# Strassen's scheme for three quarters of an MLP's up projections in a two-layer diffusion step

## The chip, the cores and the metric

The kernel runs on one core of a Trainium2 chip. Its time is the device time of one execution in microseconds; the median of the runs is compared.

## The reference, cut to what matters

One inference step of a backbone with two trunk layers, on 640 tokens (512 latent tokens and 128 context tokens) of width 1024. Each layer has four token mixers, a gated merge, and an MLP with a squared ReLU:

```python
def squared_relu_mlp(h, w1, w2):
    return jnp.square(jax.nn.relu(h @ w1)) @ w2

x = x + gt2 * squared_relu_mlp(modulate(rms_norm(x, lw['g_mlp']), sh2, sc2), lw['w_ff1'], lw['w_ff2'])
```

`w1` is 1024 x 4096, `w2` 4096 x 1024, all in float32. The change is in `h @ w1` of the second of the two layers.

## The kernel before, in words

Channels lie on the 128 partitions and tokens along the free dimension. The 640 tokens are two halves of 320 (`HALF`), and a matmul moves one half. Float32 precision is made from three passes: each operand is a rounded high part and a low part (value minus high part), and `steps` (lines 216 to 231) does, for each of 8 chunks of 128 input channels, high x high (L226), high x low (L227) and low x high (L228). A slab of weights, 1024 inputs by 128 outputs, thus takes 8 x 3 x 2 halves = 48 matmuls of 320 columns. The trace calls the weights' parts `whi` and `wlo`, those of the MLP's input `hhi` and `hlo`, those of the hidden values `hh` and `hl`.

The weights come in one order, written down at the start by `plan` in the queue `feed`. `raw` (L167) starts the load of the next slab on SyncE's queue. `prefetch` (L174) makes a loaded slab's parts: the cast to the high part on ScalarE (L192), the subtract for the low part on VectorE (L193), and then it starts the next load. `take` (L198) hands out a ready slab and, through `look`, prepares one more. There are two buffers for prepared slabs: one in use by TensorE, and the next.

The MLP splits the 4096 hidden channels into four parts (`NQ`) of eight slabs (`QJ`). The order is: up of part 0, then for q = 1, 2, 3 up of part q and down of part q-1, then down of part 3. In `up` a slab takes, after its matmuls, four steps for each half: relu from PSUM on ScalarE (L1066), square on VectorE (L1067), and the split into high part on ScalarE (L240) and low part on VectorE (L241). The first two slabs of part 0 (`first`) are done in `Norm.second`, between the last steps of the norm. In `down` a half's result is added to x on VectorE by two operations (`residual`, L1008). The down of part 3 goes through `boundary`, which does the first token halves of all eight slabs, then the second halves with the final norm between them. The chunks of a down slab are the eight hidden slabs of the part, in order.

In the merge and the MLP, the instructions of VectorE, ScalarE, GpSimd and SyncE stand in the order in which the program issues them (`in_order`); TensorE's do so everywhere. PSUM has eight banks, one for a half's result.

Of the kernel before, what the change touches and what calls it, by code (L numbers as in the profile page):

```python
# [9 lines left out]
F32 = mybir.dt.float32  # L10
F32R = mybir.dt.float32r
AF = mybir.ActivationFunctionType
ALU = mybir.AluOpType
# [15 lines left out]
NQ = 4  # L29
QJ = DFF // NQ // P  # L30
# [42 lines left out]
def hsl(h):  # L73
    return slice(h * HALF, (h + 1) * HALF)


def _r(ap):
    return ap.bitcast(F32)


class Net:
    def __init__(self, ctx, nc, tc, t):
        self.nc, self.tc, self.t = nc, tc, t
        self.uid = 0
        pool = lambda name, **k: ctx.enter_context(tc.tile_pool(name=name, bufs=1, **k))
        self.cst = pool("cst", side="left")
        self.wp = pool("wp", side="left")
        self.hp = pool("hp", side="left")
        self.dr = pool("dr", space=DRAM)
        self.ydram = [self.dr.tile([10, P, NTOK], F32, name=f"ydram{l}") for l in range(DEPTH)]  # L90
        self.gdram = [self.dr.tile([len(EARLY_GATES[l]), P, NTOK], F32, name=f"gdram{l}") for l in range(DEPTH)]
        self.xdram = self.dr.tile([P, KC, NTOK], F32, name="xdram")
        self.pv = None
        self.wm = deque()
        self.feed, self.raws, self.ready = deque(), deque(), deque()
        for l in range(DEPTH):
            self.plan(l)
# [35 lines left out]
    def plan(self, l):  # L133
        t, f = self.t, self.feed
        wa = lambda c: f.append((t["wa"][l, c], KC, P, "w", True))
        gates = iter(EARLY_GATES[l])
        slabs = [GK, GQ, GV]
        for task in FILL[l]:
            slabs += task[1] + (GATE,) * task[2] if task else (GATE,)
        assert slabs.count(GATE) == len(EARLY_GATES[l])  # L140
        for c in slabs:
            if c == GATE:
                f.append((t["wg"][l][next(gates)], KC, P, "w", True))
            elif c == MKR:
# [12 lines left out]
        for j in range(KC):  # L157
            f.append((t["wo"][l, j], KC, P, "w", False))
        up = lambda q: [f.append((t["w1"][l, q * QJ + j], KC, P, "w", False)) for j in range(QJ)]
        down = lambda q: [f.append((t["w2"][l, q, j], KC, P, "w", False)) for j in range(KC)]  # L160
        up(0)
        for q in range(1, NQ):
            up(q)
            down(q - 1)
        down(NQ - 1)

    def raw(self):  # L167

        src, kc, m, tag, eng = self.feed.popleft()
        r = self.wp.tile([P, kc, m], F32, name="raw" + tag, tag="raw" + tag, bufs=2 if tag == "w" else 1)  # L170
        self.nc.sync.dma_start(r, src.rearrange("p (k m) -> p k m", k=kc))
        self.raws.append((r, kc, m, tag, eng))

    def prefetch(self, dst=None):  # L174

        nc = self.nc
        if not self.raws:
            self.raw()
        raw, kc, m, tag, eng = self.raws.popleft()
        if dst is None:  # L180
            hi, lo = (self.wp.tile([P, kc, m], F32R, name=n + tag, tag=n + tag, bufs=2 if tag == "w" else 1)
                      for n in ("whi", "wlo"))
        else:
            hi, lo = dst
        if eng and kc == KC:

            for a, e in ((0, nc.gpsimd), (KC // 2, nc.vector)):
                c = slice(a, a + KC // 2)
                nc.scalar.copy(hi[:, c], raw[:, c])  # L189
                e.tensor_tensor(lo[:, c], raw[:, c], _r(hi[:, c]), ALU.subtract)  # L190
        else:
            nc.scalar.copy(hi, raw)  # L192
            nc.vector.tensor_tensor(lo, raw, _r(hi), ALU.subtract)  # L193
        while self.feed and not self.raws or self.raws and self.feed and self.raws[-1][3] != "w" and self.feed[0][3] == "w":
            self.raw()
        self.ready.append((hi, lo, tag))

    def take(self, ahead=True, dst=None):  # L198

        if not self.ready:  # L200
            self.prefetch()
        hi, lo, tag = self.ready.popleft()
        if ahead:
            self.look(tag)
        return hi, lo

    def look(self, last="w"):

        while self.raws or self.feed:
            if self.ready:  # L210
                last = self.ready[-1][2]
                if last == "w":
                    return
            if last == "b" and (self.raws[0][3] if self.raws else self.feed[0][3]) == "b":
                return
            self.prefetch()
# [823 lines left out]
    def mlp(self, l, x, first):  # L1040
# [52 lines left out]
            down(q - 1)  # L1093
        down(NQ - 1)

    def start(self):

        nc, t = self.nc, self.t
        self.ps_stack = ExitStack()
        self.ps_stack.enter_context(self.psum(8))  # L1100
        xs = ExitStack()
        xp = xs.enter_context(self.tc.tile_pool(name="xp0", bufs=1, side="right"))
        self.ccol = xp.tile([P, KC, 2], F32, name="ccol")
        cc = self.ccol.rearrange("p k v -> p (k v)")
        nc.sync.dma_start(cc, t["ccol"])
        self.silu(xp, cc, 2 * KC)
        x = xp.tile([P, KC, NTOK], F32, name="x")
        wm = []
# [24 lines left out]

        for j in range(KC + 4):
            if j < KC:
                g[j] = self.mod_first(xp, j, wm[j])
                next(g[j])
            if j in (1, 2):
                N.stat(j - 1)
            if j in (2, 3):  # L1140
                N.spread(j - 2, True)
                self.prefetch()
                ws.append(self.take(ahead=False))
                for hf in range(2):
# [12 lines left out]
        for g in st.values():  # L1157
            next(g, None)
        self.prefetch()
        N.close()  # L1160
        xs.close()
        self.first = ps

    def run(self):
        nc, tc, t = self.nc, self.tc, self.t
        with self.in_order("PE"):
            self.start()
            for l in range(DEPTH):
# [8 lines left out]
                    self.cb = [xp.tile([P, D], F32, name=f"cb{v}") for v in range(2)]  # L1177
                with self.in_order("DVE", "Activation", "Pool", "SP"):
                    self.merge(l, x)
                    self.mlp(l, x, self.first)  # L1180
                if l + 1 < DEPTH:
                    nc.sync.dma_start(self.xdram, x)
                xs.close()
# [445 lines left out]
```

## Time and profile before

| what | value |
|---|---|
| median of 3 runs | 2373.49 us (2371.53 to 2373.98) |
| the profiled execution | 2371.4 us |
| its span, first to last instruction | 2369.6 us |
| mean granted TensorE clock | 0.991 |

In the rows below PE is TensorE's matmuls, PEld its weight loads, DVE VectorE, ACT ScalarE, POOL GpSimd, SP SyncE. L12 is line 12 of the kernel. Matmuls are pipelined: the trace gives each about 0.31 us, and one starts every 0.146 us. A timeline row is start, duration, engine, line, operation, output and inputs; in brackets the idle time before it and what ended it. A row of the stretches view is the stretch, its length, the busy us (and the number of instructions) of PE, PEld, DVE, ACT and POOL, the granted clock of TensorE (1.00 is 2.4 GHz, 0.50 is 1.2), the DMA engines' busy share and GB/s. A row of grouped instructions ends with the total busy time in us, the mean of one in ns, and the idle time before them.

### The profile page before, as it was taken

To read this page: it belongs to the slowest core of one execution; us is meant where nothing else is said; L and a number is where in the kernel's file an instruction comes from. 1 tells how busy PE (TensorE), PEld (TensorE's weight loads), DVE (VectorE), ACT (ScalarE), POOL (GpSimd) and SP (SyncE) were. 2 spreads that over 40 slices of the span, in tenths; PEclk is the share of its full clock that TensorE was granted. 3 is DMA by queue.
4 is the path that set the end of the run, shared out by engine and by line. 5 is a ranking of instruction groups with operands and counts; after the bars stand their busy time and mean duration, and the time that the engine had idled before them with its cause. 6 is when DMAs were issued, how large, how long until landed. Compare 5 with 4: busy or idle time off the path is not lost. (4 is left out here: it accounts for less than half of the span.)

```text
span 2369.6 us, 39989 instructions
## 1 busy us (share of the span) xinstructions
PE 2302.6 (97%) x15766; PEld 2245.0 (95%) x15766; DVE 1391.4 (59%) x2812; ACT 935.3 (39%) x1971; POOL 418.9 (18%) x496
## 2 busy tenths in 40 slices
PE   8999999999999999999999999999999999999998
PEld 4998998899999999999999999988999999999998
DVE  5766666557765786877566656655434554343433
ACT  5555555432224332222254555554322344131311
POOL 0333333112231000000123333322113200000001
PEclk9999999999999999999999999999999999999999
DMA  6331321155541344444331323211424312222222
GB/s 241 99 104 63 104 87 66 66 202 167 174 154 61 139 162 151 160 144 159 116 135 66 110 89 103 86 66 56 170 94 134 99 54 72 80 72 78 74 81 72
DMA packets 91371, 261.33 MB, mean 110 GB/s; under 512 B 10416, under 2 KB 29232, under 8 KB 89776
## 3 DMA queue, kind: packets, MB, share of 16 engines
q1 hardware_dynamic: 91184, 258.78, 32.5%
q8 instruction: 124, 2.03, 0.3%
q14 instruction: 63, 0.52, 0.1%
HBM read 231.31 MB, written 21.92 MB: 107 GB/s over the span
## 5 line engine op out<-in xcount | busy, mean ns | idle before, releaser
L226 PE MATMUL pr<-hhi,whiw 128*128 128x320 f32 (+1 forms) x2752 | 867.8, 315 | 12.8 <-DVE y L598 3.0
L228 PE MATMUL pr<-hhi,wlow 128*128 128x320 f32 (+1 forms) x2752 | 852.2, 310 | 3.0 <-DVE wlow L193 2.1
L227 PE MATMUL pr<-hlo,whiw 128*128 128x320 f32 (+1 forms) x2752 | 852.7, 310 | 0.1
L226 PEld LDWEIGHTS pr<-hhi,whiw 128*128 128x128 f32 (+1 forms) x2752 | 516.2, 188 | 18.5 <-issue 5.6
L228 PEld LDWEIGHTS pr<-hhi,wlow 128*128 128x128 f32 (+1 forms) x2752 | 515.2, 187 | 5.8 <-DVE wlow L193 3.5
L227 PEld LDWEIGHTS pr<-hlo,whiw 128*128 128x128 f32 (+1 forms) x2752 | 516.1, 188 | 3.7 <-DVE hlo L1255 2.6
L192 ACT CAST whiw<-raww 128x1024 fp32r<-128x1024 f32 (+2 forms) x170 | 173.5, 1021 | 298.4 <-PE pr L227 269.4
L226 PE MATMUL pr<-hh,whiw 128*128 128x320 f32 x832 | 257.1, 309 | 0.0
L227 PE MATMUL pr<-hl,whiw 128*128 128x320 f32 x832 | 256.9, 309 | 0.0
L228 PE MATMUL pr<-hh,wlow 128*128 128x320 f32 x832 | 256.9, 309 | 0.0
L193 DVE TENSOR_TENSOR wlow<-raww,whiw 128x1024 fp32r<-128x1024 f32 (+2 forms) x170 | 208.2, 1225 | 61.5 <-ACT whiw L192 60.8
L1210 POOL TENSOR_TENSOR sqs<-sqs,sq 128x320 f32<-128x320 f32 x48 | 47.7, 993 | 972.1 <-ACT sq L1208 944.4
L1008 DVE SCALAR_TENSOR_TENSOR x<-pr,mod,x 128x256 f32<-128x256 f32 x320 | 107.7, 379 | 188.8 <-PE pr L228 186.5
L553 POOL TENSOR_SCALAR p<-p,sm 128x512 f32<-128x512 f32 (+3 forms) x160 | 120.9, 756 | 400.2 <-DVE sm L552 357.7
L548 ACT ACTIVATE p<-S,sm 128x641 f32<-128x641 f32 (+6 forms) x160 | 112.1, 701 | 156.8 <-DVE sm L539 80.0
L981 POOL TENSOR_TENSOR acc<-acc,sg 128x320 f32<-128x320 f32 x96 | 100.3, 1060 | 339.3 <-DVE sg L980 339.3
L226 PEld LDWEIGHTS pr<-hh,whiw 128*128 128x128 f32 x832 | 156.4, 188 | 0.0
L227 PEld LDWEIGHTS pr<-hl,whiw 128*128 128x128 f32 x832 | 156.4, 188 | 0.0
L228 PEld LDWEIGHTS pr<-hh,wlow 128*128 128x128 f32 x832 | 156.4, 188 | 0.0
L575 DVE TENSOR_TENSOR pt<-pr,pt 128x512 fp32r<-128x512 f32 (+2 forms) x240 | 118.8, 516 | 54.2 <-ACT pt L571 52.9
L276 DVE SCALAR_TENSOR_TENSOR junk<-wm,cb 128x1024 bf16<-128x1024 f32 x112 | 136.8, 1222 | 2.0
L190 POOL TENSOR_TENSOR wlow<-raww,whiw 128x512 fp32r<-128x512 f32 (+1 forms) x72 | 94.7, 1316 | 190.9 <-ACT whiw L189 179.3
(224 smaller groups left out, 3796.2 us busy)
## 6 DMA issues: line engine op xcount, KB each, us to landing
raww<-in_w SPq DMA_DIRECT2D x128, 512.0 KB, 3.6
wm<-in_wm SPq DMA_DIRECT2D x80, 512.0 KB, 3.5
raww<-in_wg SPq DMA_DIRECT2D x64, 512.0 KB, 3.6
raww<-in_wa SPq DMA_DIRECT2D x42, 512.0 KB, 3.6
gdram<-gt SPq DMA_DIRECT2D x28, 320.0 KB, 2.2
wm<-in_wm SPq DMA_DIRECT2D x8, 1024.0 KB, 14.4
raww<-in_wo SPq DMA_DIRECT2D x16, 512.0 KB, 3.5
kt<-kt SPq DMA_DIRECT2D x24, 224.0 KB, 4.8
```

The source lines that it names most:

```text
L190: e.tensor_tensor(lo[:, c], raw[:, c], _r(hi[:, c]), ALU.subtract)
L192: nc.scalar.copy(hi, raw)
L193: nc.vector.tensor_tensor(lo, raw, _r(hi), ALU.subtract)
L226: nc.tensor.matmul(out, lhsT=whi[:, kw, :], rhs=xhi[:, kx, sl], start=(i == 0), stop=False)
L227: nc.tensor.matmul(out, lhsT=whi[:, kw, :], rhs=xlo[:, kx, sl], start=False, stop=False)
L228: nc.tensor.matmul(out, lhsT=wlo[:, kw, :], rhs=xhi[:, kx, sl], start=False, stop=(i == n - 1))
L276: nc.vector.scalar_tensor_tensor(self.junk, raw, 1.0, self.cb[v], ALU.mult, ALU.mult, accum_out=self.mod[l]["mod"][:, v, i:i + 1])
L548: nc.scalar.activation(p[:, :B["n"]], B["sc"], AF.Exp, bias=sm[:, 0:1], scale=-1.0, accum_out=sm[:, 1:2])
L553: nc.gpsimd.tensor_scalar(p[:, :n], p[:, :n], sm[:, 1:2], 1.0, ALU.mult, ALU.mult)
L575: self.nc.vector.tensor_tensor(lo, src, _r(hi), ALU.subtract)
L981: nc.gpsimd.tensor_tensor(a, a, sg, ALU.add)
L1008: self.nc.vector.scalar_tensor_tensor(x[:, j, o + a:o + b], ps[:, a:b], m[:, v, g0 + j:g0 + j + 1], x[:, j, o + a:o + b], ALU.mult, ALU.add)
```

## The change

Only the up projections of parts 1, 2 and 3 of the second layer change. A part's eight slabs make four units of two slabs. The unit's weights are four blocks (two slabs by two halves of the input channels, `a11` to `a22`), its input four blocks (two halves of the channels by two halves of the tokens), and the four result blocks come from seven block products, in a form of Strassen's scheme with few additions. A block product is 4 chunks x 3 passes = 12 matmuls of 320 columns.

- *Weights* (`parts`): the loads of such a pair go to a pool of their own with three buffers. Four steps of preparation stand for the two of before; they make seven half slabs' high and low parts (512 columns each) and four sums of blocks on VectorE. Part 1 gives a11 and a sum, part 2 two sums, part 3 a sum and a12, part 4 a22 alone. One `take` prepares one of them. The third step starts the next load.
- *Input* (`sums`): four combinations T1 to T4 of the input's blocks, with high and low parts, for each of four chunks. A call does one chunk: 14 operations on VectorE and 4 on ScalarE. The calls come after slabs 1, 3, 4 and 6 of part 0.
- *Results* (`unit`): three PSUM banks X, Y, Z. X goes on accumulating over four products, and three snapshots of X and Y are copied to SBUF (`keep`, ScalarE). Three of the four results are sums of a bank and a snapshot (`add`, VectorE). The relu, square and split of a unit are eight steps in the queue `post`, which the next unit or the next down slabs issue.
- *Order*: `plan` puts one unit ahead of the down of the part before, and three behind it. In part 0 (`plain`) the square moves from VectorE to ScalarE. The hidden parts are kept in five buffers of two slabs in place of two of eight. The boundary's spare weights lie in T1 and in the room of the MLP's input.

The core of the diff (the lines left out are allocations, the tail of `plan`, and index helpers):

```diff
         up(0)
         for q in range(1, NQ):
-            up(q)
+            up(q, 0, 2 if fast else QJ)
             down(q - 1)
+            up(q, 2 if fast else QJ, QJ)
         down(NQ - 1)
...
     def prefetch(self, dst=None):
 
         nc = self.nc
+        if self.unit:
+            self.unit.popleft()()
+            return
         if not self.raws:
             self.raw()
         raw, kc, m, tag, eng = self.raws.popleft()
+        if tag == "u":
+            self.unit = deque(self.parts(raw, self.raws.popleft()[0]))
+            self.unit.popleft()()
+            return
...
+    def parts(self, r1, r2):
+
+
+        nc, K = self.nc, KC // 2
+        a11, a12, a21, a22 = r1[:, :K], r1[:, K:], r2[:, :K], r2[:, K:]
+        sums = {}
+
+        def add(n, a, b):
+            w = sums[n] = self.upool.tile([P, K, P], F32, name="sw", tag="sw", bufs=2)
+            nc.vector.tensor_tensor(w, a, b, ALU.add)
+            return w
+
+        def put(*ops):
+            hi, lo = (self.wp.tile([P, KC, P], F32R, name=n, tag=n, bufs=2) for n in ("whiw", "wlow"))
+            for i, a in enumerate(ops):
+                c = slice(i * K, (i + 1) * K)
+                nc.scalar.copy(hi[:, c], a)
+                nc.vector.tensor_tensor(lo[:, c], a, _r(hi[:, c]), ALU.subtract)
+            self.ready.append((hi, lo, "w"))
+
+        def third():
+            put(add(3, a11, a21), a12)
+            if self.feed and not self.raws:
+                self.raw()
+
+        return [lambda: put(a11, add(1, a21, a22)),
+                lambda: put(add(2, sums[1], a11), add(4, sums[2], a12)),
+                third, lambda: put(a22)]
...
+        def sums(k):
+
+            tt = nc.vector.tensor_tensor
+            (b11, l11), (b12, l12), (b21, l21), (b22, l22) = (
+                [_r(a[:, kb * K + k, hsl(n)]) for a in h] for kb in range(2) for n in range(2))
+
+            def diff(a, la, b, lb):
+                r, d = tmp(), tmp()
+                tt(r, a, b, ALU.subtract)
+                tt(d, la, lb, ALU.subtract)
+                tt(r, r, d, ALU.add)
+                return r
+
+            def put(n, r, sign=1.0):
+                hi, lo = (a[:, k] for a in T[n])
+                nc.scalar.activation(hi, r, AF.Copy, scale=sign)
+                nc.vector.scalar_tensor_tensor(lo, r, sign, _r(hi), ALU.mult, ALU.subtract)
+
+            put(3, diff(b22, l22, b12, l12))
+            r = diff(b11, l11, b12, l12)
+            put(1, r)
+            for b, op in ((b22, ALU.add), (l22, ALU.add)):
+                tt(r, r, b, op)
+            put(2, r, -1.0)
+            for b in (b21, l21):
+                tt(r, r, b, ALU.subtract)
+            put(4, r)
...
+            w = self.take()
+            mm(X, w, 0, B(0, 0), True, True)
+            keep("a", X)
+            mm(Y, w, 1, T[1], True, True)
+            keep("d", Y)
+            run(1)
+            w = self.take()
+            mm(X, w, 0, T[2], False, True)
+            keep("b", X)
+            run(2)
+            mm(Y, w, 1, B(1, 1), False, True)
+            c12 = add(Y, "b")
+            run(2)
+            w = self.take()
+            mm(X, w, 0, T[3], False, True)
+            n22 = add(X, "d")
+            run(2)
+            mm(Z, w, 1, B(1, 0), True, True)
+            c11 = add(Z, "a")
+            run(1)
+            w = self.take()
+            mm(X, w, 0, T[4], False, True)
+            assert not post
...
+            def second():
+                nc.vector.scalar_tensor_tensor(n22, n22, 0.0, n22, ALU.min, ALU.mult)
+                hi(1, 1, n22)
+
+            def fourth():
+                r21.append(tmp())
+                relu(r21[0], X[:, :HALF], -1.0)
+                hi(1, 0, r21[0])
+
+            post.extend([lambda: (relu(c12, c12, 1.0), hi(0, 1, c12)), lambda: lo(0, 1, c12), second,
+                         lambda: lo(1, 1, n22), lambda: (relu(c11, c11, 1.0), hi(0, 0, c11)),
+                         lambda: lo(0, 0, c11), fourth, lambda: lo(1, 0, r21[0])])
+
+        for j in range(QJ):
+            ps = first[j] if j < 2 else None
+            if ps is None:
+                w = self.take()
+                ps = [self.half(w, h, hf) for hf in range(2)]
+            plain(0, j, ps)
+            if j in (1, 3, 4, 6):
+                sums({1: 0, 3: 1, 4: 2, 6: 3}[j])
+        for q in range(1, NQ):
+            unit(q)
+            a = part(q - 1)
+            for j in range(KC):
+                w = self.take()
+                for hf in range(2):
+                    self.residual(l, x, j, hf, self.half(w, a, hf), 40)
+                run(1)
+            for _ in range(QJ // 2 - 1):
+                unit(q)
+        run(len(post))
...
-                    self.mlp(l, x, self.first)
+                    (self.mlp if l + 1 < DEPTH else self.mlp_fast)(l, x, self.first)
```

In `mm` the twelve matmuls of a block run chunk by chunk, high x high, high x low, low x high, so a block wants the low weights with its third matmul. `relu` is two operations on ScalarE (relu, then square), `hi` a cast on ScalarE, `lo` a subtract on VectorE, and `run(n)` issues the next n steps of `post`.

## Rows read from the trace of the kernel before

**Rows 1.** The page's busy times: us, share of the span, instructions.

```profile
PE 2302.6 (97%) x15766; PEld 2245.0 (95%) x15766; DVE 1391.4 (59%) x2812; ACT 935.3 (39%) x1971; POOL 418.9 (18%) x496
```

**Rows 2.** Stretches view, middle of layer 1's MLP.

```profile
2100.00:2200.00 100.00, 100.00 (x684) 100.00 (x684) 40.51 (x72) 25.36 (x39) 0.00 (x0) 1.00 0.24 77
```

**Rows 3.** Waits, 1900 to 2369 us: total us, times, longest us.

```profile
ACT whiw L192 <- PE pr L227: 126.7, 22, 6.0
PE pr L228 <- DVE wlow L193: 0.7, 1, 0.7
```

**Rows 4.** Groups by line and shape, 1900 to 2369 us.

```profile
L193 DVE TENSOR_TENSOR wlow<-raww,whiw 128x1024 fp32r<-128x1024 f32 x56 | 68.6, 1226 | 22.2 <-ACT whiw L192 22.2
L241 DVE TENSOR_TENSOR hl<-fr,hh 128x320 fp32r<-128x320 f32 x64 | 31.5, 492 | 33.6 <-ACT hh L240 33.6
L240 ACT CAST hh<-fr 128x320 fp32r<-128x320 f32 x64 | 29.4, 460 | 37.9 <-DVE fr L1067 37.9
L1066 ACT ACTIVATE fr<-pr 128x320 f32<-128x320 f32 x64 | 28.0, 438 | 94.1 <-PE pr L228 94.1
```

**Rows 5.** Groups by line and shape, whole span.

```profile
L193 DVE TENSOR_TENSOR wlow<-raww,whiw 128x512 fp32r<-128x512 f32 x7 | 4.8, 684 | 0.0
L192 ACT CAST whiw<-raww 128x512 fp32r<-128x512 f32 x7 | 4.2, 604 | 0.0
L856 ACT COPY st<-pr 128x320 f32<-128x320 f32 x8 | 3.4, 419 | 1.1 <-PE pr L228 1.1
```

**Rows 6.** VectorE's timeline, the norm and part 0's start.

```profile
1908.29 0.49 DVE L1255 TENSOR_TENSOR hlo<-nt,hhi 128x320 fp32r<-128x320 f32 x1
1908.70 0.48 DVE L1249 TENSOR_TENSOR nt<-x,pr 128x320 f32<-128x320 f32 x1
1909.21 0.32 DVE L1252 TENSOR_SCALAR nt<-nt,modsc,mod 128x64 f32<-128x64 f32 x1
...
1924.58 0.49 DVE L241 TENSOR_TENSOR hl<-fr,hh 128x320 fp32r<-128x320 f32 x1 [0.53 <-ACT hh L240]
1925.53 1.22 DVE L193 TENSOR_TENSOR wlow<-raww,whiw 128x1024 fp32r<-128x1024 f32 x1 [0.46 <-ACT whiw L192]
```

**Rows 7.** ScalarE's timeline in the first slabs of part 0.

```profile
1918.04 0.43 ACT L1066 ACTIVATE fr<-pr 128x320 f32<-128x320 f32 x1
...
1919.82 0.46 ACT L240 CAST hh<-fr 128x320 fp32r<-128x320 f32 x1 [1.35 <-DVE fr L1067]
1920.19 0.43 ACT L1066 ACTIVATE fr<-pr 128x320 f32<-128x320 f32 x1
...
1924.45 1.04 ACT L192 CAST whiw<-raww 128x1024 fp32r<-128x1024 f32 x1
1925.40 0.43 ACT L1066 ACTIVATE fr<-pr 128x320 f32<-128x320 f32 x1
...
1930.40 0.44 ACT L1066 ACTIVATE fr<-pr 128x320 f32<-128x320 f32 x1 [0.38 <-PE pr L228]
```

**Rows 8.** TensorE's timeline, slab 3 of part 0.

```profile
1926.81 0.41 PE L228 MATMUL pr<-hhi,wlow 128*128 128x320 f32 x1
...
1930.14 0.31 PE L226 MATMUL pr<-hhi,whiw 128*128 128x320 f32 x1
```

**Rows 9.** Stretches view, around a wait in layer 1's mixers.

```profile
1492.00:1493.00 1.00, 0.00 (x0) 0.00 (x0) 0.93 (x4) 0.98 (x6) 0.10 (x1) 1.00 0.41 130
...
1495.00:1496.00 1.00, 1.00 (x8) 0.82 (x6) 0.97 (x4) 0.00 (x0) 0.28 (x1) 0.60 0.00 0
1496.00:1497.00 1.00, 1.00 (x6) 1.00 (x5) 0.94 (x4) 0.76 (x2) 0.00 (x0) 0.50 0.03 10
1497.00:1498.00 1.00, 1.00 (x6) 1.00 (x5) 0.97 (x2) 0.27 (x1) 0.76 (x1) 0.50 0.83 318
1498.00:1499.00 1.00, 1.00 (x7) 1.00 (x7) 0.56 (x2) 0.67 (x1) 0.00 (x0) 0.70 0.89 250
```

**Rows 10.** DMA issues, 1900 to 2369 us: KB each, median us to landing.

```profile
raww<-in_w SPq DMA_DIRECT2D x60, 512.0 KB, 3.5
```

More of the change, by code (lines that the diff above doesn't have):

```diff
@@ L93, in __init__ @@
         self.pv = None
-        self.wm = deque()
+        self.wm, self.unit = deque(), deque()
         self.feed, self.raws, self.ready = deque(), deque(), deque()
@@ L158, in plan @@
             f.append((t["wo"][l, j], KC, P, "w", False))
-        up = lambda q: [f.append((t["w1"][l, q * QJ + j], KC, P, "w", False)) for j in range(QJ)]
+        fast = l == DEPTH - 1
+        up = lambda q, a=0, b=QJ: [f.append((t["w1"][l, q * QJ + j], KC, P, "u" if fast and q else "w", False))
+                                   for j in range(a, b)]
         down = lambda q: [f.append((t["w2"][l, q, j], KC, P, "w", False)) for j in range(KC)]
@@ L169, in raw @@
         src, kc, m, tag, eng = self.feed.popleft()
+        if tag == "u":
+            for a in (src, self.feed.popleft()[0]):
+                r = self.upool.tile([P, kc, m], F32, name="rawu", tag="rawu", bufs=3)
+                self.nc.sync.dma_start(r, a.rearrange("p (k m) -> p k m", k=kc))
+                self.raws.append((r, kc, m, tag, eng))
+            return
         r = self.wp.tile([P, kc, m], F32, name="raw" + tag, tag="raw" + tag, bufs=2 if tag == "w" else 1)
@@ L179, in prefetch @@
         raw, kc, m, tag, eng = self.raws.popleft()
+        if tag == "u":
+            self.unit = deque(self.parts(raw, self.raws.popleft()[0]))
+            self.unit.popleft()()
+            return
         if dst is None:
@@ L207, in look @@
     def look(self, last="w"):
-        while self.raws or self.feed:
+        while self.raws or self.feed or self.unit:
             if self.ready:
@@ L1094, in mlp, with mlp_fast, hidden, __init__ @@
         down(NQ - 1)
+    def mlp_fast(self, l, x, first):
+        nc, tc = self.nc, self.tc
+        s = ExitStack()
+        fp = s.enter_context(tc.tile_pool(name="fp", bufs=1, side="right", reuse_waits="tile"))
+        us = ExitStack()
+        self.upool = us.enter_context(tc.tile_pool(name="up", bufs=1, side="right", reuse_waits="tile"))
+        K = KC // 2
+        hid = {q: [] for q in range(NQ)}
+        h = self.h
+        T = {n: [fp.tile([P, K, HALF], F32R, name=f"T{n}{p}") for p in "hl"] for n in range(1, 5)}
+        B = lambda k, n: [a[:, k * K:(k + 1) * K, hsl(n)] for a in h]
+        tmp = lambda: fp.tile([P, HALF], F32, name="fr", tag="fr", bufs=4)
+        post = deque()
+        def hidden(q):
+            hid[q].append([fp.tile([P, 2, NTOK], F32R, name=n, tag=n, bufs=5) for n in ("hh", "hl")])
+            return hid[q][-1]
+        def sums(k):
[21 more added lines that the diff above has]
+            put(4, r)
+        class Chunks:
+            def __init__(self, tiles):
+                self.tiles = tiles
+            def __getitem__(self, i):
+                return self.tiles[i[1] // 2][i[0], i[1] % 2, i[2]]
+        part = lambda q: [Chunks([u[p] for u in hid[q]]) for p in range(2)]
+        def plain(q, j, ps):
+            hh, hl = hid[q][-1] if j % 2 else hidden(q)
+            for hf in range(2):
+                r = tmp()
+                nc.scalar.activation(r, ps[hf][:, :HALF], AF.Relu)
+                nc.scalar.activation(r, r, AF.Square)
+                self.split(hh[:, j % 2, hsl(hf)], hl[:, j % 2, hsl(hf)], r)
+        def mm(ps, w, i, b, start, stop):
+            n = 0
+            for k in range(K):
+                for wp, bp in ((0, 0), (0, 1), (1, 0)):
+                    nc.tensor.matmul(ps[:, :HALF], lhsT=w[wp][:, i * K + k, :], rhs=b[bp][:, k], start=start and n == 0,
+                                     stop=stop and n == 3 * K - 1, skip_group_check=not start)
+                    n += 1
+        def run(n):
+            for _ in range(min(n, len(post))):
+                post.popleft()()
+        def unit(q):
+            X, Y, Z = (self.bank() for _ in range(3))
+            snap = {}
+            def keep(n, ps):
+                c = snap[n] = fp.tile([P, HALF], F32, name="sn", tag="sn", bufs=3)
+                nc.scalar.copy(c, ps[:, :HALF])
+            def add(ps, n):
+                c = tmp()
+                nc.vector.tensor_tensor(c, ps[:, :HALF], snap[n], ALU.add)
+                return c
+            w = self.take()
[21 more added lines that the diff above has]
+            assert not post
+            hh, hl = hidden(q)
+            r21 = []
+            relu = lambda r, a, sign: (nc.scalar.activation(r, a, AF.Relu, scale=sign),
+                                       nc.scalar.activation(r, r, AF.Square))
+            hi = lambda i, hf, r: nc.scalar.copy(hh[:, i, hsl(hf)], r)
+            lo = lambda i, hf, r: nc.vector.tensor_tensor(hl[:, i, hsl(hf)], r, _r(hh[:, i, hsl(hf)]), ALU.subtract)
+            def second():
[21 more added lines that the diff above has]
+                w = self.take()
+                for hf in range(2):
+                    self.residual(l, x, j, hf, self.half(w, a, hf), 40)
[3 more added lines that the diff above has]
+        run(len(post))
+        us.close()
+        gh, gl = (self.hp.tile([P, KC, NTOK], F32R, name=n, tag=n).rearrange("p k n -> p (k n)") for n in ("hhi", "hlo"))
+        cut = lambda a, i: a[:, i * D:(i + 1) * D].rearrange("p (k m) -> p k m", k=KC)
+        dst = [tuple(cut(a.rearrange("p k n -> p (k n)"), 0) for a in T[1])]
+        dst += [(cut(gh, i), cut(gl, i)) for i in range(5)]
+        self.boundary(l, x, part(NQ - 1), dst, 40, None, s)
```

## The prediction

> **What bounds it now.** Read the busy times of the profile's page first: TensorE is busy for 97% of the span [rows 1]. The table of stretches then says how: in the middle of layer 1's MLP every 100 us hold 684 matmuls at the full clock [rows 2], so one 320-column matmul costs 0.1462 us, one slab of weights (48 matmuls) 7.02 us, and VectorE and ScalarE are busy for 40% and 25%. The view of who waited for whom says that this is a true bound: over the whole MLP of layer 1 the weight casts wait 126.7 us for TensorE, while TensorE waited for low weights once, for 0.7 us [rows 3]. So TensorE sets the end, and what it saves is saved, as long as the other engines stay ahead of it. They stay ahead by one slab only: `take` prepares one slab while TensorE works on the one before.
>
> **What is removed.** A unit does 7 block products of 12 matmuls where two slabs took 8. 12 units x 12 matmuls x 0.1462 us = **21.0 us**, all on the bounding engine. The rest is what VectorE and ScalarE get to do, and where it stands in their queues.
>
> **Prices.** VectorE: 320 columns 0.49 us, 512 columns 0.68, 1024 columns 1.23; ScalarE: relu from PSUM 0.44, cast of 320 0.46 (I take it for square and relu from SBUF too), copy of a bank 0.42, cast of 512 0.60, of 1024 1.04 [rows 4, 5, 7]. Neighbours that don't depend on each other start earlier than that: VectorE after 0.41 (1908.29 to 1908.70), where one needs the other's result after 0.51 [rows 6]; ScalarE after 0.37 (1919.82 to 1920.19), after 0.95 for 1024 columns [rows 7]. For 512 columns I take 0.61 and 0.53 from these. ScalarE starts 0.26 us after the next half's first matmul (1930.14 to 1930.40) [rows 7, 8]; the other hand-overs are 0.03 to 0.06. Both engines work in program order: the next slab's cast (1924.45) and subtract (1925.53) come only behind the last hidden half (1924.58) [rows 6, 7], and so it will be for everything put between.
>
> [...]
>
> **Part 0: the four `sums`.** Each has 14 VectorE operations of 320 columns and 4 ScalarE roundings, and VectorE waits for each rounding before the low half. From its start: two subtracts at 0 and 0.41, the dependent add at 0.93 to 1.42, rounding 1.44 to 1.90, low half 1.94; the next three roundings start at 3.80, 5.75 and 7.70 by the same steps. It stands between the hidden half of slab j and the weights of slab j+2: their cast starts at 8.07, the subtract ends at 10.37. The sums themselves start 2.13 after slab j's end (0.26, then relu, square and cast 1.42, then the low half 0.04 and 0.41). So slab j+2 has its low weights 2.13 + 10.37 + 0.06 = 12.56 us after slab j's end, and TensorE wants them with its third matmul, 7.02 + 0.29 = 7.31 after it: **5.2 us of standing still**, for j = 3 and for j = 4 alike (there the sums start behind the late casts of slab 5, with the same result). For j = 6 the first thing behind is a unit's half slab, ready at 9.90: 4.8 us. For j = 1 four hidden halves come one after another, each 1.33 on ScalarE from 1918.04 [rows 7]; the sums start at 1923.90, the low weights are there at 1934.3, and TensorE took them at 1926.81 [rows 8]: 7.5 us. Together **22.7 us lost**, more than the whole saving. Nothing hides it: the cover was the one slab.
>
> Where TensorE stood still (1492 to 1493 without a matmul), the granted clock went to 0.50, its lower level, soon after, and came back by 1499: 0.4 + 0.5 + 0.5 + 0.3 = 1.7 us of time lost [rows 9]. I take that for each of the four stalls; behind two of them (slab 5 and the first unit) the next wait for VectorE takes it up, the other two cost **3.4 us**. By the Trainium skill (TensorE: Matmul & The Clock Gate, "HAM oscillation") a matmul stream that waits falls to half rate and pays for it after each wait, which speaks against this change; the rows agree, but by the rule all four would be paid, 6.8 us.
>
> **The units.** TensorE needs 84 x 0.1462 = 12.28 us for one. VectorE has 11 operations of 512 columns and 8 of 320: 10.0 us at the pitches above; ScalarE 7 of 512 and 13 of 320, with the waits inside relu, square and cast 9.2. Both fit, but hand over to each other in a fixed order. Follow a unit from the start of `n22 = add(X, "d")` (0): low half, `c11`, low half, `add(1)` at 1.64, the low half of the next unit's a11 at 2.25, done 2.93. TensorE's last block (0.55 to 2.31) is through, and the next unit's third matmul waits 0.4 for it; its two first blocks end at 6.21. ScalarE copies Y ("d") at 6.47, then in its queue relu, square, cast of the last unit's c12, the casts of part 3 (8.16, 8.69), and only then copies X ("b", 9.22). VectorE goes on with part 3's low halves (8.81, 9.42), a low half (10.03), `second` (10.44 to 10.93); ScalarE casts that at 10.96, does c11's three, and at 12.68 to 13.29 part 4's weights; their low half on VectorE (13.33) stands in front of the next `n22`: **13.94**. So a unit in a row of units takes 13.9 us against 14.03 for two slabs before, and all but 0.1 of its 1.75 goes into TensorE's waits (0.4 for a11, 1.2 for `n22` before the last block). A unit behind eight down slabs finds the queues empty and takes 12.3. The second slab of a pair is loaded when part 3 is through (10.1) and lands 3.5 us later [rows 10], 1.5 before `add(1)` reads it: no cost, but little cover.
> The order is one unit, 8 downs, 3 units + 1, 8 downs, 3 + 1, 8 downs, 3. The first unit stands behind the last sums and two hidden halves: 14.6. Then 54.0 + 54.0 (12.3 + 3 x 13.9 each) + 39.7 (12.3 + 13.9 + 13.5). Together 162.3 against 12 x 14.03 = 168.4: the units **gain 6.1 us**. Bounds: 21 us gained if TensorE never waits, 9 us lost if each of the nine waits longer by the 1.65 us that the chain would have without overlapping starts.
>
> **The end.** The last unit's eight late steps run at once in front of the last part's first down slab: ScalarE's part is 4.5 us, and that slab's seventh and eighth chunk want them 3 us after it starts: **2 us lost**. The 8 downs elsewhere take one step each, in idle time.
>
> **Sum.** -21.0 is contained in the units; 22.7 + 3.4 - 6.1 + 2.0 = +22.0 us on the profiled execution's 2371.4, which lies 2.1 under the median of the runs. On the median 2373.5: **2395.5 us**.
>
> **Rivals.** *The added work is hidden* (faster). It needs the four sums to stall TensorE little and the units to run at its pace. The least that the rows allow for the sums is 14 x 0.41 with the roundings free: the low weights are then there 6.96 us after the start in place of 10.37, the stalls 4.1 + 1.8 + 1.8 + 1.9 = 9.6 us. With units at 12.28 (-21.0) and the end's 2.0 this gives -9.4: 2364 us. It decides the sign from stalls under 19 us on. For it: busy sums of 10.0 and 9.2 in 12.28. Against it: in the kernel before VectorE waits for ScalarE's cast at each hidden half and each slab [rows 6], and the order of the queues is the same. *No overlapping starts* (slower still): if VectorE and ScalarE start each operation only when the last has ended, the sums grow by nine pitches of 0.53 for 0.41, 1.1 us each (+4.3) and nine units by 1.65 (+14.9): 2415 us. VectorE's part alone gives +4.3 and nine times 0.93: 2408 us. The overlaps in [rows 6, 7] speak against both. [...] *Half of it*: the sums stall half as long, because VectorE starts a low half's neighbours while it still waits for the rounding, and the units gain as forecast: 11.4 + 0 - 6.1 + 2.0 = +7; with the units 5 us better, +2. Around 2378 us; against it speaks the wait of each low half in its place [rows 6].
>
> **Chances.** Forecast 0.73; hidden 0.08; no overlap 0.11 (0.05 of it for VectorE alone); half 0.08, a good half of that within 0.2% of no change. A measurement of this kernel can tell some 0.2%, 4.7 us. So faster 0.08, same 0.05, slower 0.87. The range takes the forecast with its own unknowns (units 8 us to either side, clock 0 to 6.8, sums 4) and most of the slower case: 2383 to 2411.
>
> **What would show it.** In the profile after: about 144 matmuls fewer; in part 0 four waits of TensorE on the low weights, one of some 7.5 and three near 5 us, with the granted clock at half behind them; VectorE nearly full there; units of 12.3 behind downs and near 13.9 in a row, with TensorE waiting on a DVE add before each unit's last block. The prediction is wrong in its main step if slabs 3, 5, 6 start without such waits; wrong in size if the units in a row take 12.5 or 15.5.

## The result and the profile after

The changed kernel takes **2400.6 us** (median of 4 runs, 2394.9 to 2405.6) against 2372.5 for the kernel before on the same chips: ratio **1.012, 95% interval 1.0094 to 1.0146**, slower, at the place that was forecast (2395.5, range 2383 to 2411). The profiled execution of after took 2405.6 us.

The page of after, span and busy times, against [rows 1]:

```profile
span 2403.8 us, 40008 instructions
...
PE 2304.4 (96%) x15622; PEld 2238.4 (93%) x15622; DVE 1460.2 (61%) x2960; ACT 997.2 (41%) x2123; POOL 418.6 (17%) x496
```

144 matmuls fewer, and yet TensorE is no less busy in sum: over the span its granted clock was 0.983 in place of 0.991, and a matmul at the lower clock takes longer (0.63 in the rows of the waits below, 0.31 at the full one). The waits of TensorE from layer 1's MLP to the end, kernel after (total us, times, longest), against [rows 3], where there was one wait of 0.7 us on a low weight:

```profile
PE pr L272 <- ACT whiw L209: 14.4, 4, 6.9
PE pr L1212 <- DVE fr L1230: 8.7, 8, 1.1
PE pr L1212 <- ACT whiw L231: 3.9, 1, 3.9
PE pr L274 <- DVE wlow L210: 3.2, 7, 0.7
PE pr L1212 <- DVE wlow L232: 1.4, 6, 0.3
```

L209 and L210 make a slab's parts, L231 and L232 a unit's, L1212 is the matmul of a block, L1230 the add of bank and snapshot. Up to layer 1's MLP both programs are the same, yet the executions that were profiled reach its first matmul at different times (1900.54 us before, 1907.94 after; the ten experiments from 1896 to 1908). So I compare **the stretch from that matmul to the end of the span**: 2369.6 - 1900.54 = 469.1 us before, 2403.8 - 1907.94 = 495.9 after, **+26.8** (forecast: +22.0).

TensorE's timeline of after, the four places in part 0 and at the first unit where it stood still:

```profile
1940.70 0.63 PE L272 MATMUL pr<-hhi,whiw 128*128 128x320 f32 x1 [6.86 <-ACT whiw L209]
1941.96 0.63 PE L274 MATMUL pr<-hhi,wlow 128*128 128x320 f32 x1 [0.36 <-DVE wlow L210]
...
1962.40 0.63 PE L272 MATMUL pr<-hhi,whiw 128*128 128x320 f32 x1 [4.29 <-ACT whiw L209]
1963.66 0.63 PE L274 MATMUL pr<-hhi,wlow 128*128 128x320 f32 x1 [0.36 <-DVE wlow L210]
...
1974.87 0.41 PE L272 MATMUL pr<-hhi,whiw 128*128 128x320 f32 x1 [2.65 <-ACT whiw L209]
1976.13 0.41 PE L274 MATMUL pr<-hhi,wlow 128*128 128x320 f32 x1 [0.70 <-DVE wlow L210]
...
1995.58 0.64 PE L1212 MATMUL pr<-hhi,whiw 128*128 128x320 f32 x1 [3.87 <-ACT whiw L231]
1996.80 0.64 PE L1212 MATMUL pr<-hhi,wlow 128*128 128x320 f32 x1 [0.32 <-DVE wlow L232]
```

They are slabs 3, 5, 6 and the first unit, the four that stand two slabs behind a `sums`. From where the slab's third matmul would have been it is late by 8.0, 5.4, 3.8 and 5.0 us. VectorE's timeline of after shows why, in the sums behind slab 1:

```profile
1930.87 0.49 DVE L287 TENSOR_TENSOR hl<-fr,hh 128x320 fp32r<-128x320 f32 x1 [0.84 <-ACT hh L286]
1931.28 0.48 DVE L1170 TENSOR_TENSOR fr<-hhi 128x320 f32<-128x320 f32 x1
...
1932.20 0.49 DVE L1172 TENSOR_TENSOR fr<-fr 128x320 f32<-128x320 f32 x1
1933.23 0.49 DVE L1178 SCALAR_TENSOR_TENSOR T3l<-fr,T3h 128x320 fp32r<-128x320 f32 x1 [0.54 <-ACT T3h L1177]
...
1935.58 0.49 DVE L1178 SCALAR_TENSOR_TENSOR T1l<-fr,T1h 128x320 fp32r<-128x320 f32 x1 [0.54 <-ACT T1h L1177]
1936.11 0.49 DVE L1184 TENSOR_TENSOR fr<-fr,hhi 128x320 f32<-128x320 f32 x1
...
1939.74 0.49 DVE L1178 SCALAR_TENSOR_TENSOR T4l<-fr,T4h 128x320 fp32r<-128x320 f32 x1 [0.54 <-ACT T4h L1177]
1940.68 1.23 DVE L210 TENSOR_TENSOR wlow<-raww,whiw 128x1024 fp32r<-128x1024 f32 x1 [0.44 <-ACT whiw L209]
```

The sums run from 1931.28 to 1940.23, each low half 0.54 behind its rounding, and slab 3's low weights, in the same queue, come after them. The stretches of after show the price of standing still (the granted clock is the third column from the end, 0.50 its lower level; compare [rows 9]):

```profile
1930.00:1940.00 10.00, 3.84 (x27) 3.57 (x25) 6.81 (x16) 2.97 (x7) 0.00 (x0) 0.82 0.00 0
1940.00:1950.00 10.00, 8.94 (x42) 8.54 (x43) 4.16 (x6) 5.49 (x11) 0.00 (x0) 0.67 0.31 105
...
1960.00:1970.00 10.00, 7.24 (x34) 6.85 (x35) 6.91 (x14) 4.88 (x10) 0.00 (x0) 0.66 0.43 158
```

The stretch in pieces, from the same timelines: part 0 to the first unit's third matmul 27.3 us over before; units 5.0 under the twelve pairs of slabs, which took 14.08 us each (first unit from its third matmul 14.7, then 54.47, 54.44 and 40.31); the three downs behind units 1.3 over; the last part 3.2 over. Together +26.8.

### The profile page after: what moved, and what is told of

It reads as the page before. It is cut to its first block, busy times and chain, and to the rows that moved or that the text cites. A ratio compares the mean times of both kernels' runs of the same rounds, so it can differ in the third digit from the quotient of the medians.

```text
span 2403.8 us, 40008 instructions
## 1 busy us (share of the span) xinstructions
PE 2304.4 (96%) x15622; PEld 2238.4 (93%) x15622; DVE 1460.2 (61%) x2960; ACT 997.2 (41%) x2123; POOL 418.6 (17%) x496
## 5 line engine op out<-in xcount | busy, mean ns | idle before, releaser
L272 PE MATMUL pr<-hhi,whiw 128*128 128x320 f32 x2368 | 753.2, 318 | 27.3 <-ACT whiw L209 15.1
L274 PE MATMUL pr<-hhi,wlow 128*128 128x320 f32 x2368 | 736.8, 311 | 4.4 <-DVE wlow L210 3.5
L273 PE MATMUL pr<-hlo,whiw 128*128 128x320 f32 x2368 | 737.3, 311 | 0.1
L272 PEld LDWEIGHTS pr<-hhi,whiw 128*128 128x128 f32 x2368 | 447.1, 189 | 33.8 <-ACT whiw L209 16.7
L274 PEld LDWEIGHTS pr<-hhi,wlow 128*128 128x128 f32 x2368 | 446.1, 188 | 7.9 <-DVE wlow L210 5.7
L273 PEld LDWEIGHTS pr<-hlo,whiw 128*128 128x128 f32 x2368 | 447.1, 189 | 3.7 <-DVE hlo L1461 2.6
L209 ACT CAST whiw<-raww 128x1024 fp32r<-128x1024 f32 (+2 forms) x146 | 148.2, 1015 | 243.2 <-PE pr L273 207.8
L210 DVE TENSOR_TENSOR wlow<-raww,whiw 128x1024 fp32r<-128x1024 f32 (+2 forms) x146 | 178.8, 1224 | 52.8 <-ACT whiw L209 52.4
```

The lines of the kernel that those rows point to most:

```text
L272: nc.tensor.matmul(out, lhsT=whi[:, kw, :], rhs=xhi[:, kx, sl], start=(i == 0), stop=False)
L273: nc.tensor.matmul(out, lhsT=whi[:, kw, :], rhs=xlo[:, kx, sl], start=False, stop=False)
L274: nc.tensor.matmul(out, lhsT=wlo[:, kw, :], rhs=xhi[:, kx, sl], start=False, stop=(i == n - 1))
```

## The experiments

Times are of single runs unless an interval stands with them; "stretch" is the one above.

**Leave out the sums** (`e1_no_sums`). T1 to T4 are filled with zeros once by GpSimd, and the four calls are gone: the input's combinations are not computed.

```diff
+        for n in T:
+            for a in T[n]:
+                nc.gpsimd.memset(_r(a), 0.0)
...
-            if j in (1, 3, 4, 6):
-                sums({1: 0, 3: 1, 4: 2, 6: 3}[j])
```

> Leaves out the four sums: T1 to T4 are filled with zeros once by GpSimd. Theory (the sums, queued ahead of the next slab's weights on VectorE, cost part 0 its time): the stretch from the MLP's first matmul to the first unit's falls from 87.6 us to about 61.5, the first unit (15.7) comes to 12.5, the units in rows stay at 14.1; the run is some 29 us below the changed kernel's 2400.6, about 2372. Rival (the units themselves cost it): part 0 is at most 5 us shorter and the run stays above 2392.

Measured: 2366.5 us, stretch 468.6, 27.3 under the changed kernel. Part 0 60.9, first unit 13.5, units in a row still 14.1. The waits on L209 and L231 are gone from the table, while the waits before the last block stay:

```profile
PE pr L1212 <- DVE fr L1230: 8.8, 8, 1.1
```

So the sums cost all of the loss, and the units' saving about cancels the rest. (The gain would be 1.5 more but for the last part, which ran at a lower clock here; see the last section.)

**The next weights ahead of the sums** (`e2_weights_first`).

```diff
-                w = self.take()
+                w = w or self.take()
                 ps = [self.half(w, h, hf) for hf in range(2)]
+                w = None
             plain(0, j, ps)
             if j in (1, 3, 4, 6):
+                w = self.take()
                 sums({1: 0, 3: 1, 4: 2, 6: 3}[j])
```

> The next slab's weights are prepared ahead of the sums instead of behind them; nothing else. Theory (VectorE's volume with its waits for the roundings is the cost, the place only says which slab pays): the wait moves one slab on, behind the hidden halves that now stand behind the sums; from the rows' durations waits of 5, 3 and 6 us in part 0 and 7 us in the first unit, so part 0 and the first unit together stay within 5 us of the 103.3 they take, and the run within 5 us of 2400. Rival (the place alone): the weights are in time, all four waits go, the run falls by some 25 us to 2376.

Measured: 2399.4 us, stretch 489.6; part 0 77.5 and the first unit 19.5, together 97.0 against 103.3, 1.3 us more of a change than the theory allowed. The rival, by which all the waits were the weights' place in the queue, falls: ScalarE stays behind the last rounding of each sum with the next relu and the next cast, so the wait comes back one slab later (9.7 us on the casts, 5.0 on the first unit's copy of a bank). One slab's weights ahead is not a cure while the sums of a chunk stay one block.

**Matmuls in the waits** (`e3_filler`). Matmuls with an unused result are put where TensorE stood still, so that it doesn't stop.

```diff
+        fill = {2: 42, 4: 30, 5: 32, 7: 28}
...
+            if j in fill:
+                dummy = self.bank()
+                for _ in range(fill[j]):
+                    nc.tensor.matmul(dummy[:, :HALF], lhsT=h[0][:, 0, 0:P], rhs=h[0][:, 0, hsl(0)], start=True, stop=True)
             plain(0, j, ps)
```

> TensorE does matmuls that nobody reads (42, 30, 32 and 28 of 320 columns) in the four waits of part 0. Theory (two of the four stretches at the lower clock lie on the path): the granted clock stays at 1.00 through part 0, slabs 3 and 6 end 2.1 and 1.6 us earlier, part 0 takes about 84 us for 87.6, the run 4 us less. Rival (the clock costs nothing that the next wait doesn't take up): part 0 stays at 87 to 88. If the fillers themselves overrun the waits: longer.

Measured: 2391.4 us, stretch 492.4, **3.5 less**, with 132 matmuls more; part 0 took 84.2 us and ran at a granted clock of 1.00 throughout. The low clock costs what two of the four stalls were priced at (3.4). It also shows where the other two went. TensorE's timeline of e3, slab 5's last matmul and slab 6's third:

```profile
1957.62 0.31 PE L274 MATMUL pr<-hhi,wlow 128*128 128x320 f32 x1
...
1963.40 0.41 PE L274 MATMUL pr<-hhi,wlow 128*128 128x320 f32 x1 [0.49 <-DVE wlow L210]
```

At the full clock slab 6's third matmul is 5.3 us late, for 3.8 in the changed kernel; the other three are as late as there (8.0, 5.4, 5.0), and the first unit takes 15.6 for 15.7. So what the low clock cost in slab 5 and in the first unit was taken up by the next wait.

**Part 4's weights ahead of two late steps** (`e4_part4_first`), in a unit's order of ScalarE's queue:

```diff
             c12 = add(Y, "b")
-            run(2)
             w = self.take()
+            run(3)
             mm(X, w, 0, T[3], False, True)
             n22 = add(X, "d")
-            run(2)
+            run(1)
...
-                         lambda: lo(1, 1, n22), lambda: (relu(c11, c11, 1.0), hi(0, 0, c11)),
+                         lambda: (relu(c11, c11, 1.0), hi(0, 0, c11)), lambda: lo(1, 1, n22),
```

> In a unit, part 4's weights are prepared ahead of the relu, square and cast of the last unit's c11 instead of behind them. Theory (the units in a row are set by the order of ScalarE's queue, through part 4's low half in front of the add that frees X): a unit in a row takes 13.6 us for 14.13, the nine of them 4.5 us less; the wait before the last block falls from 1.1 to about 0.6. Rival (VectorE's or ScalarE's pace sets them, whatever the order): 14.1 as before.

Measured: 2396.1 us, stretch 492.4, 3.5 less. A unit in a row takes 13.47 us; in the changed kernel the second unit of a run took 13.65 and the later ones 14.13. The wait before the last block shrinks:

```profile
PE pr L1212 <- DVE fr L1230: 7.2, 8, 0.9
```

The order of the queues bears on a unit's time, as the chain in the prediction had it; that it sets all of it is shown by g3 below.

**GpSimd takes the weights' adds** (`f1_pool_adds`), and the same with a unit's late steps spread over more slots of the next one, no more than two in a slot (`f2_orderB_pool`, whose further edit isn't shown):

```diff
             w = sums[n] = self.upool.tile([P, K, P], F32, name="sw", tag="sw", bufs=2)
-            nc.vector.tensor_tensor(w, a, b, ALU.add)
+            nc.gpsimd.tensor_tensor(w, a, b, ALU.add)
```

> The four weight-block adds of a unit go from VectorE to GpSimd; all orders stay. VectorE's queue is then some 2 us shorter per unit, but the order of the late steps on ScalarE, which sets the wait before the last block, stays. Theory (ScalarE's order and VectorE's late low halves share the 14.1 us of a unit in a row): about 13.6 us per unit in a row, 4 us less in the stretch from the MLP's first matmul to the end (492). Rival 1 (VectorE's load alone sets it): 12.3 per unit, 15 less (481). Rival 2 (GpSimd's 128x512 operations at 1.34 us make the weights late): 14.5 or more, stretch above 497.

> As f1_pool_adds, and the late steps of a unit are spread one by one between the blocks of the next one, each put where its engine is free, so that neither the copies of the products nor the weights' roundings queue behind three ScalarE steps in a row. Theory (it is the order, not the amount of work): units in a row at TensorE's own pace, 12.3 to 12.6 us, stretch 480 to 483, 13 to 16 below the changed kernel. Rival (the engines beside TensorE have too much work for 12.3 us): 13.4 or more, stretch above 490.

Measured: 2405.0 us (stretch 502.6) and 2405.2 (502.7), 6.7 and 6.8 us **slower** than the changed kernel; units in a row 14.1 to 15.1, and 13.3 to 16.1. Both theories missed; f1's second rival (GpSimd's adds make the weights late) and f2's were right on the time, but not by GpSimd's own duration or VectorE's load alone. Of f1's 6.7 us the runs of units lost 4.5, the rest is part 0's and the last part's. VectorE's groups by shape, from about the first run of four units to the last unit; the kernel after, then f1:

```profile
L232 DVE TENSOR_TENSOR wlow<-sw,whiw 128x512 fp32r<-128x512 f32 x43 | 29.5, 692 | 18.1 <-ACT whiw L231 17.0
...
L1261 DVE TENSOR_TENSOR hl<-fr,hh 128x320 fp32r<-128x320 f32 x45 | 21.8, 485 | 3.3 <-ACT hh L1260 2.2
L1230 DVE TENSOR_TENSOR fr<-pr,sn 128x320 f32<-128x320 f32 x33 | 16.1, 488 | 8.9 <-PE pr L1212 8.1
```

```profile
L232 DVE TENSOR_TENSOR wlow<-sw,whiw 128x512 fp32r<-128x512 f32 x43 | 32.9, 786 | 34.6 <-ACT whiw L231 34.6
L1261 DVE TENSOR_TENSOR hl<-fr,hh 128x320 fp32r<-128x320 f32 x41 | 26.4, 645 | 1.0
...
L1230 DVE TENSOR_TENSOR fr<-pr,sn 128x320 f32<-128x320 f32 x33 | 16.1, 487 | 10.3 <-PE pr L1212 9.4
```

VectorE's operations on two SBUF operands grew on average from 692 to 786 and from 485 to 645 ns; the add that reads one operand from PSUM did not (488, 487). How the loss divides between these longer operations and casts that wait for GpSimd's adds was not tried.

**GpSimd takes the forty additions of the sums** (`f3_pool_sums`; ScalarE and VectorE keep the roundings and low halves, behind slabs 1, 2, 4 and 5), and that with the edits of f2 (`f4_all`):

```diff
-            tt = nc.vector.tensor_tensor
...
+            tt = nc.gpsimd.tensor_tensor
...
+        when = {1: 0, 2: 1, 4: 2, 5: 3}
...
-            if j in (1, 3, 4, 6):
-                sums({1: 0, 3: 1, 4: 2, 6: 3}[j])
+            if j in when:
+                sums(when[j])
```

> The forty subtractions and additions of the operand sums go to GpSimd, which is idle there, from the start of the part on; ScalarE and VectorE keep only the rounding and the low half of each sum, after slabs 1, 2, 4 and 5. Theory (VectorE's chains of additions stand ahead of the weights' low halves): part 0 falls from 87.6 to between 61 and 64 us, stretch 469 to 473. Rival (GpSimd and VectorE slow each other where they work side by side, or the roundings alone make the weights late): part 0 above 72 us, stretch above 480. Units as in the changed kernel, 14.1 in a row.

> f2_orderB_pool and f3_pool_sums together. If the two costs are independent, the gains add: stretch 453 to 458, 11 to 16 below the kernel before (469.1). Rival (GpSimd's work of the sums delays the first unit's weight adds, and the gains overlap): 460 or more.

Measured: 2383.1 us (stretch 478.7) and 2386.1 (481.7). In f3 part 0 took 71.3 us, between theory and rival, and the first unit 13.4; f4 came out on its rival's side (460 or more), as f2's part of it is a loss and no gain. The gain of 17.2 us is two thirds of what the sums cost (63%), and behind the rest one finds the two engines in each other's way. VectorE's timeline of f3, then GpSimd's beside it:

```profile
1952.56 0.49 DVE L287 TENSOR_TENSOR hl<-fr,hh 128x320 fp32r<-128x320 f32 x1 [2.53 <-ACT hh L286]
1952.97 1.17 DVE L1193 SCALAR_TENSOR_TENSOR T3l<-rawu,T3h 128x320 fp32r<-128x320 f32 x1
1954.06 1.17 DVE L1193 SCALAR_TENSOR_TENSOR T1l<-rawu,T1h 128x320 fp32r<-128x320 f32 x1
```

```profile
1952.63 1.16 POOL L1176 TENSOR_TENSOR rawu<-hhi 128x320 f32<-128x320 f32 x1
1953.76 1.13 POOL L1177 TENSOR_TENSOR sn<-hlo 128x320 f32<-128x320 f32 x1
```

An operation of VectorE that takes 0.49 alone takes 1.17 beside GpSimd's, and both start one every 1.1 us: they take turns.

**All on VectorE, in another order** (`g3_both`). The differences of a chunk are made one part at a time, always behind the next slab's weights (T1, T2, T4 behind slabs 1, 3, 4, 5; T3 of two chunks behind slabs 2 and 6); a unit's late steps become fifteen single operations in `post` (`c`: relu, square, high, low part of c12; `n`: min-square, high, low of n22; `d` as `c` for c11, `f` for X), issued two behind each of the three copies, three behind c12, two behind part 4's weights, four behind n22; the last unit makes first what the last downs read first.

```diff
-            post.extend([lambda: (relu(c12, c12, 1.0), hi(0, 1, c12)), lambda: lo(0, 1, c12), second,
-                         lambda: lo(1, 1, n22), lambda: (relu(c11, c11, 1.0), hi(0, 0, c11)),
-                         lambda: lo(0, 0, c11), fourth, lambda: lo(1, 0, r21[0])])
...
+            post.extend(d + f + c + n if q == NQ - 1 and len(hid[q]) == QJ // 2 else [c[0], n[0], f[0], c[1], c[2], c[3], n[1], d[0], n[2], d[1], d[2], d[3], f[1], f[2], f[3]])
```

> The changed kernel with its added work re-ordered and nothing put on another engine. Part 0: a slab's worth of the sums at a time on VectorE (the differences of T1, T2, T4 of one chunk behind slabs 1, 3, 4, 5, those of T3 two at a time behind slabs 2 and 6), always behind the next slab's weights. Units: the late steps in fifteen single operations between the blocks, VectorE's and ScalarE's apart. Last unit: the half that the last down part reads first comes first, the other half is finished beside the downs. Theory (the cost was order, not amount): part 0 61 to 65 us (changed kernel 87.6), units in a row 12.3 to 12.7 (14.1), downs as they were, last part 58 to 60 (61.4), stretch from the MLP's first matmul to the end 451 to 456 against 469.1 before and 495.9 changed, time 2353 to 2360, ratio to the kernel before 0.992 to 0.995. Rival (VectorE is full where the added work is, whatever its order: 6.9 us of work per slab of 7.0, 11.5 per unit of 12.3): units 13.4 or more and part 0 above 70, stretch 466 or more, ratio 0.998 or above.

Measured, 5 rounds: 2370.6 us, ratio to the kernel before **0.9996 (0.9983 to 1.0008)**: the loss is gone, no more. The units did what theory said, 12.31 to 12.34 us in a row; part 0 took 67.8 us, between theory and rival, and the first unit 21.5. The waits of g3 in part 0 and the first unit, all engines:

```profile
ACT T1h L1185 <- DVE fr L1174: 10.5, 4, 2.6
ACT T3h L1185 <- DVE fr L1174: 6.4, 4, 2.6
...
PE pr L1223 <- ACT sn L1237: 5.9, 1, 5.9
```

ScalarE stands still behind roundings whose sums VectorE is still making, with the next slab's relu and weight cast behind them, and the first unit's copy of its first product stands behind slab 7's steps and T3's roundings.

**The same, with the roundings one slab later** (`h1_pipelined`). T4's and T3's rounding wait in `post` until the next slab's hidden values are out, and slab 7's own steps go into the first unit's slots.

```diff
+            if third:
+                r3 = diff(held(), b22, l22, b12, l12)
+                post.append(lambda: put(3, r3))
+                return
...
-            put(4, r)
...
+            post.append(lambda: put(4, r4))
```

> As g3_both, whose units ran at 12.31 us in a row (theory) while its part 0 took 67.1 us and its first unit 21.5. There ScalarE stood still behind the rounding of each chunk's last sum, up to 2.6 us at a time, with the next slab's relu and weight rounding queued behind it (a slab with sums took 9.1 us), and the first unit's copy of its first product stood behind slab 7's steps (5.9 us). Now the rounding of T4 and of T3 is emitted one slab later, when VectorE has long made the sum; slab 7's relu, square, rounding and low half, and the last T4 rounding, go between the blocks of the first unit. Theory (latency of the two engines' turns, not their load): part 0 61.5 to 64 us, first unit 12.3 to 13.8, stretch 453 to 457 against 469.1 before, 12 to 16 us less than the kernel before, ratio 0.993 to 0.996. Rival (VectorE's load of about 6.9 us per slab of 7.0 is the limit, and any shift only moves the wait): part 0 and first unit together above 84 (88.7 in g3_both), stretch above 464, ratio above 0.998.

Measured, 5 rounds: 2357.1 us against 2373.8, ratio **0.9932 (0.9914 to 0.995)**, faster than both kernels. Stretch 456.2; part 0 61.8 us, the kernel before 61.3; first unit 14.7, over the 12.3 to 13.8 that were expected; units in a row 12.31. Waits of TensorE in the stretch, and the stretches of part 0 and of the first run of four units, kernel h1:

```profile
PE pr L1226 <- ACT sn L1240: 2.1, 1, 2.1
PE pr L274 <- DVE wlow L210: 1.7, 6, 0.7
```

```profile
1902.05:1963.80 61.75, 60.19 (x404) 58.32 (x403) 47.85 (x102) 40.41 (x83) 0.00 (x0) 1.00 0.21 69
...
2035.32:2084.79 49.47, 49.47 (x339) 49.26 (x337) 39.96 (x72) 31.90 (x69) 0.00 (x0) 1.00 0.24 75
```

VectorE is busy for 47.9 of 61.8 us and 40.0 of 49.5, with the same 2960 instructions as in the changed kernel: the change's cost was the order of its added work. Against the kernel before the stretch is 12.9 us shorter: units -18.1, part 0 +0.5, downs +1.4, last part +3.3. Of this last one the waits at the last part's start went (downs 59.9 in place of the changed kernel's 61.4), but the tail behind them took 13.3 us in place of 11.6, at a clock of 0.58 in place of 0.72; why it fell lower there was not tried.

## Why the prediction was right

- **What bounds it.** Right: without the sums (e1) and with the same units the kernel is at the time of before, and in h1 the units run at 12.31 for 84 matmuls, 0.1465 each: TensorE's pace.
- **Part 0, the sums.** Forecast 7.5 + 5.2 + 5.2 + 4.8 = 22.7 us of standing still; measured 8.0, 5.4, 3.8, 5.0 = 22.2 at the clock as it was, and 8.0, 5.4, 5.3, 5.0 = 23.8 at the full clock (e3), for which the forecast was worked out. Each chain was about 0.3 us longer than worked out, because an add in place waits for the low half before it (1935.58 to 1936.11, 0.53, where 0.41 was taken). The third stall is shorter in the changed kernel because slab 5 ran 1.7 us longer at the low clock, which is time that VectorE had too.
- **The clock.** Forecast 3.4, measured 3.5 by the experiment that takes it away, and hidden behind slab 5 and the first unit, the two places that were named. (Counted in the changed kernel alone it is 27.3 less 22.2, 5.1, with slab 5's part out of the third stall.) By the rule of the Trainium skill that was set against it (TensorE: Matmul & The Clock Gate, "HAM oscillation") it would have been 6.8; the trace agrees that the clock falls behind each of the long waits (0.71, 0.76, 0.82 and 0.73 in the 48 matmuls behind them), but what it cost behind two of them the next wait took up (e3).
- **The units.** The chain was right for a row: 13.65, 14.13 and 14.13 where 13.94 stood, and the wait before the last block is 1.1, as forecast (1.2); e4 moved steps of it and gained 0.2 us on the second unit of a run and 0.66 on the later ones. Behind downs a unit took 12.54 for 12.3, so the units took 163.9 us for 162.3. A pair of slabs takes 14.08 and not 14.03: the 684 of [rows 2] counts matmuls that only overlap the ends of the 100 us, while the starts of two parts of eight slabs lie 56.32 us apart, 0.1467 a matmul. So the units gain 5.0, and with the 0.4 that each of the three down parts behind them lost, 3.7 where 6.1 stood.
- **The end.** Forecast 2.0, measured 3.2: the second down slab's low weights were late too (0.70), which the step had left out.
- **A sign that did not come.** VectorE was to be nearly full in part 0; it was busy for 52.0 of 87.6 us. It stood still behind the roundings, which is what the chain says: the stalls came from the order of the steps and not from a full engine.
- **The rivals.** *Hidden*: VectorE's load did fit, as its busy sums said, and h1 reaches 2357 us, below the 2364 of that rival, but in another order of work; in the order of the change it was wrong. *No overlapping starts*: wrong, neighbours start 0.41 apart (1930.87 to 1931.28), as in [rows 6]; its price counts nine units in a row where the sum of the units has eight (3 + 3 + 2), 1.65 us too much (0.93 for VectorE alone). *Half of it*: wrong, each low half waits 0.54 in its place.

The sum came to +22.0 for +26.8: the stalls were 1.1 too small, the clock 0.1, the units with their downs gained 2.4 less, and the end cost 1.2 more.

## What to carry to other kernels

When a change saves work on the bounding engine and puts work on engines that have room, ask of each added step what stands behind it in its queue and by when that is due; busy shares don't tell (VectorE at 60% lost 22 us here, and the same instructions in another order lost none). Cut added work into pieces shorter than the cover, put them behind the step that feeds the bounding engine, and issue the other engine's half of a hand-over one round later, so that neither queue stands still waiting for its partner. Moving work to an idle engine costs more than that engine's time where the two take turns at the same memory: four adds a unit made this kernel slower, and forty operations in part 0 kept two thirds of what the sums cost.

## What was not expected

GpSimd and VectorE, working side by side on SBUF operands, slow each other to taking turns: 0.49 to 1.17 us for 128x320 with f32 operands, 1.22 to 1.90 for the weights' 128x1024, and GpSimd's own 0.88 to as much as 1.74 (f3), while VectorE's operation with a PSUM operand kept its 487 ns. The averages of f1 hide how sharp this is: by the timelines, ten of L1261's low halves ran beside an operation of GpSimd (for 0.1 us or more) and took 1143 ns on average, the other 35 took 484; and thirteen of L1230's adds with a PSUM operand also ran beside one and took 488. The Trainium skill says so (SBUF — State Buffer, "SBUF: two separate sides"): the two share a pair of ports as an exclusive lock, which an operation of VectorE with two SBUF inputs takes for its whole duration; the trace agrees, on both sides of the condition.

The same short waits at the start of the last part (the longest 0.2, 0.2 and 0.7 us) left the clock at 1.00 in the changed kernel and at 0.97 in e1 and f3, where the last downs took 1.5 and 1.3 us longer (63.0 and 62.8 for 61.4); why is open. And executions of one and the same stretch ahead of the MLP ended up to 12 us apart, more than most of the effects here: without a stretch of their own the experiments could not have been told apart.
